# Layer 0 of a hybrid trunk: another split of the small inverses over the partitions, a written DMA order, and factors begun earlier

## The chip, the cores and the metric

The kernel runs on one core of one Trainium2 chip. The core has a matrix engine (TensorE, here PE), a vector engine (VectorE, DVE), a scalar engine (ScalarE, ACT), a slower general engine (GpSimd, POOL) and a queue that issues transfers (SyncE, SP). Each works off its own instructions in order, and they meet through semaphores. Transfers are done by 16 DMA engines. The metric is the device time of one execution in microseconds (us); lower is better.

## What is computed

Two layers run over 512 prompt tokens and 32 sample tokens (T = 544 columns). Layer 0 is an RWKV-7 mixer, layer 1 differential attention. Each layer also attends to a memory of 256 rows, gates its output and projects it back. Layer 0 is where the change lies. For each of 24 heads, reference and kernel follow the recurrence

```python
def step(S, inp):
    r_t, k_t, v_t, w_t, kk_t, a_t = inp
    sa = jnp.einsum('bhvk,bhk->bhv', S, -kk_t)
    S = (S * w_t[:, :, None, :] + sa[..., None] * (kk_t * a_t)[:, :, None, :]
         + v_t[..., None] * k_t[:, :, None, :])
    return S, jnp.einsum('bhvk,bhk->bhv', S, r_t)
```

with r, k, v, w, kk and a taken from the projection `h @ rw_in` (1024 rows) and its shift by one token. Afterwards come a group norm, the gate `silu`, and `x + out @ w_out`.

## The kernel before

**Tiling.** The 24 heads are handled as 12 pairs (128 partitions each). Tokens are cut into chunks of 64: eight for the prompt, a ninth for the sample. Inside a chunk the recurrence becomes matrix products, which need the inverse of a triangular 64x64 matrix per head and chunk. It is built from 32x32 blocks: 32 blocks per pair for the prompt and 2 for the sample, 34 in all (`NBLK`).

**Stages of a pair**, each a generator that is advanced one segment at a time by `go(kind, pr)`:

- `prep` (`rw_prep`): from the projections k, r, v it makes the decays, the factors `zr` and `bk`, the products `at` and `ats` (PE, tiles `ps_at`, `ps_ats`), and writes the blocks to be inverted to a scratch in device memory (`sc1`, L637 and L639). From there it loads them three times into `m3` (L641), once for each of three classes of rows.
- `inv` (`rw_invert`): POOL inverts all blocks together. `m3`, `u3` and `tm` are tiles of 3x34 = 102 partitions; 62 instructions (L689, L691) on tiles of falling size, after a copy of the unit matrix into `u3` (L683).
- `back` (`rw_back`): `u3` goes to a scratch `sc2` (L699, three transfers), and from there into `at` (L706) and `ats` (L708).
- `mrg` (`rw_merge`): DVE transposes blocks of `at` into `t1b`; PE makes `ps_w` from them (two rounds), which joins 32x32 inverses into 64x64 ones.
- `val`, `chain`, `smp`, `out`, `fin`: products with v, the eight chunks one after the other (three segments each, called hops below: PE, DVE, PE, ACT, PE, DVE, with psum tile `ps_c`), the sample's chunk, the outputs and the group norm.

**Dense work.** All projections (k, r, v, gates, queries, memory) run as blocks of 48 PE instructions on `ps_g` (24 for a memory block). A value is split into a high and a low half (`whi`, `wlo`), and three products are added up. `stream()` yields these blocks one instruction at a time. At the start of block i it issues the load of block i+2 (`raw`, L262) and puts the splitting of block i+1 on a list of put-off work, which `some()` takes from.

**Order.** While `self.ordered` is set, the instructions of PE, DVE and ACT are tied to program order (`Queue`, `tie`); transfers and POOL are not, and the framework's scheduler places them. Before the first chain there is a ramp: `FILL0` and `FILL1` say how many dense instructions follow each segment of `prep` of pairs 0 and 1 (384 in the whole ramp). Then for each pair there are 23 steps of one hop each, and `PLAN` says what else goes into the two halves of each step: (kind, which pair counted from this one, PE time, DVE time). The dense instructions left for the pair (192 in most, 144 in pair 0, 96 in pair 9, 240 in pairs 10 and 11) are spread evenly over planned PE time.

What matters below of the `PLAN` before, by step: `inv` of the next pair at step 1, `back` at step 13, `mrg` at 18, 19 and 21. `prep` of the pair after next begins at step 0, reaches `ats` at step 20, and its last four segments are taken in the next pair.

Of the kernel before, what the change touches and what calls it, by code (L numbers as in the profile page):

```python
# [33 lines left out]
RKV = 5  # L34
# [11 lines left out]
    [[("val", 0, 1.1, 0)], [("prep", 2, 0, 0), ("fin", -1, 0, 1.0)]],  # L46
    [[("prep", 1, 0.25, 0)], [("inv", 1, 0, 0), ("fin", -1, 0, 0.84)]],
    [[("prep", 1, 0.4, 0), ("fin", -1, 0, 0)], [("prep", 2, 0, 0.6)]],
    [[("val", 0, 0.8, 0)], [("fin", -1, 0, 0.98)]],
    [[("prep", 2, 1.04, 0.17), ("out", -1, 0.11, 0)], [("prep", 1, 0.53, 0)]],  # L50
    [[("prep", 2, 0.33, 0)], [("rsq", 0, 0, 1.5)]],
    [[("prep", 2, 0.33, 0), ("prep", 1, 0.4, 0)], [("prep", 2, 0, 0.1), ("fin", -1, 0, 0.88)]],
    [[("prep", 2, 0, 1.45)], [("prep", 2, 0.33, 0)]],
    [[("prep", 2, 0.33, 0), ("fin", -1, 0.6, 1.0)], [("prep", 2, 0, 0.5)]],
    [[("prep", 2, 0.1, 0), ("prep", 2, 0, 0)], []],
    [[("prep", 2, 0, 0.42)], [("prep", 2, 0, 1.04)]],
    [[("prep", 2, 0.56, 1.0), ("smp", 0, 0.11, 0.28)], []],
    [[("prep", 2, 0, 1.0), ("smp", 0, 0.21, 0.29)], [("prep", 2, 0, 0.86)]],
    [[("prep", 2, 0, 0.84)], [("back", 1, 0, 0)]],
    [[("prep", 2, 0, 1.1), ("smp", 0, 0.21, 0)], [("fin", -1, 0, 0.73)]],  # L60
    [[("prep", 2, 0, 0.86)], []],
    [[("prep", 2, 1.1, 1.37)], []],
    [[("prep", 2, 0, 0.9)], []],
# [4 lines left out]
    [[("out", 0, 1.6, 0.7)], [("prep", 2, 0.36, 0.43)]]]  # L68
# [5 lines left out]
             + [(10.5 + k, 4) for k in range(10)]}  # L74

FILL0 = [8, 4, 10, 0, 4, 4, 10, 2, 2, 2, 2, 8, 4, 8, 8, 8, 6, 6, 8, 8, 10, 6, 10, 6, 4, 4, 4, 4, 4, 4]
FILL1 = 6
FILLE = [20, 8, 8, 8, 10, 12, 10, 8]
# [19 lines left out]
class Trunk:  # L98
# [82 lines left out]
    def consts_rwkv(self, c):  # L181
# [44 lines left out]
        self.ve.tensor_scalar(cls[:], cl[:], float(NBLK), None, ALU.is_ge)  # L226
        for k in range(2, NCL):
            cl2 = c.tile([NCL * NBLK, 1], F32, name=f"cl2{k}")
            self.ve.tensor_scalar(cl2[:], cl[:], float(k * NBLK), None, ALU.is_ge)
            self.ve.tensor_tensor(cls[:], cls[:], cl2[:], ALU.add)  # L230
# [25 lines left out]
    def load(self, src, c0):  # L256

        h = KT // 2
        raws = []
        for q in range(2):  # L260
            raw = self.wp.tile([P, h, P], F32, tag="raw", name="raw", bufs=RAWS)
            self.nc.sync.dma_start(raw[:], src[q * h * P : (q + 1) * h * P, c0 : c0 + P].rearrange("(k p) c -> p k c", p=P))  # L262
            raws.append(raw)
        return raws
# [30 lines left out]
    def some(self, room):  # L295

        us = 0.0
        if self.later and 0 < self.later[0][1] <= room:
            fn, us = self.later.pop(0)
            fn()  # L300
        if self.later and self.later[0][1] == 0:
            self.later.pop(0)[0]()
        return us
# [39 lines left out]
    def inputs(self):  # L343

        nc, a = self.nc, self.a
        with ExitStack() as ctx:
# [3 lines left out]
            for i in range(2):  # L350
                nc.sync.dma_start(xt[5 + i][:], a["mem_prompt"][0, i * P : i * P + P, :])
            parB = self.params(p, "pB", [(a[n].rearrange("l (j p) -> (l j) p", p=P), 16) for n in ("norm_w", "mem_norm_w")])
            self.early = [self.load(a["w_mem_k"][0], h * P) for h in range(NEARLY)]
            for i in range(4):
                nc.sync.dma_start(xt[i][:], a["x_prompt"][0, i * P : i * P + P, :])
            nc.sync.dma_start(xt[4][:TS, :], a["x_sample"][0])
# [39 lines left out]
            for k in range(0, KT, 2):  # L396
# [8 lines left out]
                nc.sync.dma_start(self.mscr[k // 2], mo[:])  # L405
# [74 lines left out]
    def load_up(self, pr):  # L480

        self.up = up = self.rp.tile([P, 2, P], F32, tag="r4", name="up", bufs=1)
        for q, n in enumerate(("rw_w_up", "rw_a_up")):
            for rows in (slice(0, 64), slice(64, P)):
                self.nc.sync.dma_start(up[rows, q, :], self.a[n][0, :, pr * P : pr * P + P])

    def rw_prep(self, st, rkv):
# [46 lines left out]
        self.ve.tensor_tensor_scan(cum[:, :CU], self.smask[:, :CU], cum[:, :CU], 0.0, ALU.mult, ALU.add)  # L534
        yield
# [3 lines left out]
        yield  # L539
        rr = self.rr  # L540
        self.ve.tensor_copy(rr[:, :10], self.r20[:, :10])
        self.ve.tensor_tensor(rr[:, 10:20], self.r20[:, :10], rr[:, :10].bitcast(F32), ALU.subtract)
        yield
# [5 lines left out]
        de = p.tile([P, CW], F32, tag="de", name="de", bufs=1)  # L549
        di = cum  # L550
        self.ae.activation(de[:, :CU], cum[:, :CU], AF.Exp, scale=-KAPPA)
        self.ae.activation(di[:, :CU], cum[:, :CU], AF.Exp, scale=KAPPA)
        yield
# [3 lines left out]

        kf = p.tile([P, T], F32, tag="tmp", name="kf", bufs=2)
        self.ae.activation(kf[:], ta[:], AF.Identity, bias=col(self.omka), scale=col(self.ka2))
        na = p.tile([P, T], F32, tag="tmp", name="na", bufs=2)  # L560
        self.ae.activation(na[:], ta[:], AF.Copy, bias=-0.5, scale=-0.5)
# [19 lines left out]
        for q, c0, n in ((0, 0, TP), (1, TP, TS)):  # L581
            psb = self.psm.tile([P, 512], F32, tag="m", name="ps_b")
            for i in range(4) if q == 0 else (4,):
# [3 lines left out]
                                         ALU.mult, ALU.mult)  # L587
        yield
        decayed(zr, 1, nk, de, 0)
# [12 lines left out]
        st["ats"] = ats = self.rb.tile([P, 2, 2, 64], F32, tag="ats", name="ats", bufs=2)  # L602
# [20 lines left out]
        yield  # L623
        ps = [self.psm.tile([P, 512], F32, tag="m", name="ps_ats") for _ in range(2)]
# [6 lines left out]
        st["m3"] = m3 = self.rb.tile([NCL * NBLK, 32, 32], F32, tag="m3", name="m3", bufs=1)  # L631
        sc1 = self.dp.tile([NBLK, 32, 32], F32, tag="sc1", name="sc1", bufs=2)
        for e in range(2):
            for b in range(2):
                o = (64 if e == 0 else 0) + 32 * b
                n = (e * 2 + b) * 8
                nc.sync.dma_start(sc1[n : n + 8].rearrange("b s t -> s b t"),  # L637
                                  at[o : o + 32, e, 1 - e].rearrange("p i h t -> p (i h) t")[:, :, 32 * b : 32 * b + 32])
        nc.sync.dma_start(sc1[32:34].rearrange("h s t -> s h t"), ats[64:96, 1, :, :32])  # L639
        for q in range(NCL):  # L640
            nc.sync.dma_start(m3[q * NBLK : (q + 1) * NBLK], sc1[:])  # L641
# [18 lines left out]
        for q in range(2):  # L660
            yield
            if q:
# [4 lines left out]
                for u in range(2):  # L667
                    sv[u] = self.rb.tile([P, 4, P], F32, tag="sv", name="sv", bufs=4)
# [10 lines left out]
    def rw_invert(self, st):  # L679

        nc, p, m3 = self.nc, self.rb, st["m3"]
# [11 lines left out]
    def rw_back(self, st):  # L693

        nc, u3, at, ats = self.nc, st["u3"], st["at"], st["ats"]
        sc2 = self.dp.tile([NBLK, 32, 32], F32, tag="sc2", name="sc2", bufs=2)
        for q in range(NCL):
            n = len(range(q, 32, NCL))
            d = nc.sync.dma_start(sc2[:, q : 32 : NCL, :], u3[q * NBLK : (q + 1) * NBLK, :n, :])  # L699
            self.order(d, self.te.last)  # L700
        for e in range(2):
            o = 64 if e == 0 else 0
            for b in range(2):
                n = (e * 2 + b) * 8
                u = slice(o + 32 * b, o + 32 * b + 32)
                nc.sync.dma_start(at[u, e, 1 - e].rearrange("p i h t -> p (i h) t")[:, :, 32 * b : 32 * b + 32],  # L706
                                  sc2[n : n + 8].rearrange("b s t -> s b t"))
        nc.sync.dma_start(ats[64:96, 1, :, :32], sc2[32:34].rearrange("h s t -> s h t"))  # L708
# [56 lines left out]
    def chunk(self, st, c, S, Snew):  # L765
# [17 lines left out]
        for h in range(2):  # L783
            self.ae.copy(cv[zs, H[h]], ps[H[h], 1, H[h]])
        yield
# [22 lines left out]
    def rw_sample(self, st):  # L808
# [3 lines left out]
        for h in range(2):  # L812
            nc.sync.dma_start(sl[64 * h : 64 * h + 64, 64 * h : 64 * h + 64], self.a["state_rwkv"][0, 0, 2 * pr + h])
# [20 lines left out]
    def state_out(self, S, dst):  # L834
# [7 lines left out]
        nc.sync.dma_start(dst.rearrange("h v k -> (h v) k"), so[:])  # L842
# [31 lines left out]
    def put(self, g, t):  # L874
        if not self.o1:
            self.nc.sync.dma_start(self.oscr[g // 8][:, g % 8, :], t[:])
# [47 lines left out]
    def mem_again(self, mh, ml):  # L924
# [3 lines left out]
        for k in range(KT + 2):  # L928
            if k < KT:
                mo[k] = p.tile([P, NMEM], F32, tag="memo", name="mo", bufs=2)  # L930
                self.nc.sync.dma_start(mo[k][:], self.mscr[k // 2][:, k % 2, :])
# [14 lines left out]
    def mem_out(self, i, kind, h, t, out, ps_pool, ps_tag):  # L946

        nc, p, scr = self.nc, self.mp, self.mem[i, kind][h]
        if kind == 0:
            nc.sync.dma_start(scr[:], t[:])  # L950
# [5 lines left out]
        nc.sync.dma_start(out[:, h, :].rearrange("(j p) d -> p j d", p=P), tok[:])  # L956
        if kind == 1:
            nc.sync.dma_start(scr[:].rearrange("p (j c) -> p j c", j=2), tok[:])
# [9 lines left out]
    def mem_block(self, i, kind, h, mh, ml, w, out, ps_pool, ps_tag):  # L968
# [5 lines left out]
        for k in range(KT):  # L974
            for u, x in ((0, mh), (0, ml), (1, mh)):
                end = k == KT - 1 and u == 1
                self.te.matmul(ps[:, :NMEM], w[u][:, k, :], x[:, k, :], start=k == 0 and x is mh and u == 0, stop=end)
                if end:
                    self.ae.copy(t[:], ps[:, :NMEM])
                    self.open.append(None)  # L980
                    self.put_off(lambda: self.mem_out(i, kind, h, t, out, ps_pool, ps_tag))
# [35 lines left out]
    def mem_steps(self, st, i, h, p):  # L1017
# [7 lines left out]
        nc.sync.dma_start(ct[:], a["cache_mem_k"][i, 0, :, h, :].rearrange("(j p) d -> p j d", p=P))  # L1025
        nc.sync.dma_start(mk[:], self.mem[i, 0][h][:])
        nc.sync.dma_start(mv[:], self.mem[i, 1][h][:].rearrange("p (j c) -> p j c", j=2))
        nc.sync.dma_start(cv[:], a["cache_mem_v"][i, 0, :, h, :].rearrange("(j p) d -> p j d", p=P))
# [68 lines left out]
    def w_out(self, i, p, order, consume, extra=None):  # L1097
# [3 lines left out]
        for g in order:  # L1101
            if self.o1:
                t = self.o1[g]
            else:
                t = p.tile([P, T], F32, tag="os", name="os", bufs=OSB)
                nc.sync.dma_start(t[:], self.oscr[g // 8][:, g % 8, :])
# [48 lines left out]
    def layer0(self, mem):  # L1155
# [6 lines left out]
        with ExitStack() as ctx:  # L1162
# [22 lines left out]
            def go(kind, pr):  # L1185
# [3 lines left out]
                elif 0 <= pr < NPAIR:  # L1189
                    if kind in ("inv", "back"):  # L1190
# [510 lines left out]
```

## Time and profile before

| | |
|---|---|
| median of 3 timed runs | 1698.08 us (1694.68 to 1702.46) |
| profiled execution: its own time | 1687.72 us |
| its span, first to last instruction | 1685.9 us |
| PE busy | 1495.1 us (89%) |
| DVE, ACT, POOL busy | 900.8, 820.2, 376.4 us |
| mean granted PE clock | 0.93 |

The profile is of one execution. A row of the "windows" view gives, for a stretch of time, each engine's busy us with its number of instructions, the clock granted to PE (1.00 is full), the share of the 16 DMA engines that was busy, and GB/s. A row of the "waits" view reads: engine and tile that waited, what ended the wait, us in total, number of times, longest. The chain of waits follows the work back from the end, each piece with its start and length. The columns of the SP rows are start, length, queue, line, transfer and count. Marks of the first `yt` copy on ACT date the start of each pair's chain: 161.5, 213.7, 280.7, 346.4, 412.0, ..., 671.8, 735.9, 804.6, 860.8 us for pairs 0 to 11.

### The profile page before, as it was taken

How to read it: one execution, taken by the hardware profiler on the slowest of the kernel's cores; microseconds unless marked ns; L12 is line 12 of the kernel's file. 1: busy time of each engine (PE TensorE's matmuls, PEld its weight loads, DVE VectorE, ACT ScalarE, POOL GpSimd, SP SyncE). 2: the span in 40 equal slices, each digit the busy share in tenths (PEclk: the TensorE clock that was granted, in tenths of full speed). 3: DMA queues.
4: the chain of work that ended last, by engine and by line, in shares of the span. 5: the costliest groups of instructions: out<-in, count | busy, mean ns of one | idle time of the engine just before them, and what ended most of it. 6: DMA issues, size and time to landing. Idle time of an engine off the chain costs nothing.

```text
span 1685.9 us, 32077 instructions
## 1 busy us (share of the span) xinstructions
PE 1495.1 (89%) x12112; PEld 1393.5 (83%) x12112; DVE 900.8 (53%) x2209; ACT 820.2 (49%) x2257; POOL 376.4 (22%) x843
## 2 busy tenths in 40 slices
PE   6986897797787877976998899899999999999997
PEld 6885786787777777865897899899998999989997
DVE  7562564664655655744566422654645564456533
ACT  6553563463563553642555422565446644565422
POOL 2033451642633623623500000310000100100000
PEclk9997897887987987977999999999999999999999
DMA  6422112112122121121323733523233222322321
GB/s 210 130 85 52 45 48 63 43 55 54 47 66 49 44 74 45 46 61 33 99 86 111 228 106 98 161 82 91 73 96 93 77 86 76 89 82 73 90 86 72
DMA packets 265381, 139.20 MB, mean 83 GB/s; under 512 B 56506, under 2 KB 255427, under 8 KB 265227
## 3 DMA queue, kind: packets, MB, share of 16 engines
q1 hardware_dynamic: 265226, 137.15, 28.8%
q8 instruction: 96, 1.57, 0.4%
q14 instruction: 59, 0.48, 0.1%
HBM read 110.98 MB, written 22.78 MB: 79 GB/s over the span
## 4 chain that ended last, share of the span: by engine, by line
PE 57%; POOL 18%; DMA 12%; issue 4%; DVE 3%; ACT 3%; SPq 3%; DVEq 0%; POOLq 0%; ACTq 0%
PE ps_g L95 38%; POOL u L691 9%; POOL tm L689 8%; DMA m<-sc 5%; DMA sc<-u 4%; PE ps_c L95 2%; PE ps_w L95 2%; PE ps_o L95 2%; PE ps_s L95 2%; DMA at<-sc 1%; PE ps_mm L95 1%; SPq L699 1%; PE ps_mo L95 1%; PE ps_v L95 1%; DVE wlo L95 1%
## 5 line engine op out<-in xcount | busy, mean ns | idle before, releaser
L95 PE MATMUL ps_g<-hh,whi 128*128 128x272 f32 x1808 | 550.9, 305 | 0.1
L95 PE MATMUL ps_g<-hh,wlo 128*128 128x272 f32 x1808 | 539.1, 298 | 0.2 <-DVE wlo L95 0.2
L95 PE MATMUL ps_g<-hl,whi 128*128 128x272 f32 x1808 | 538.1, 298 | 0.0
L95 DVE TENSOR_TENSOR wlo<-raw,whi 128x512 fp32r<-128x512 f32 x322 | 224.2, 707 | 259.7 <-ACT whi L95 256.2
L95 PEld LDWEIGHTS ps_g<-hh,whi 128*128 128x128 f32 x1808 | 348.2, 193 | 6.5 <-issue 0.6
L95 PEld LDWEIGHTS ps_g<-hl,whi 128*128 128x128 f32 x1808 | 347.6, 192 | 1.9
L95 PEld LDWEIGHTS ps_g<-hh,wlo 128*128 128x128 f32 x1808 | 347.2, 192 | 1.5 <-issue 0.6
L95 ACT CAST whi<-raw 128x512 fp32r<-128x512 f32 x322 | 193.5, 617 | 218.8 <-PE ps_g L95 164.1
L689 POOL TENSOR_TENSOR tm<-u,m 102x84 f32<-102x84 f32 (+23 forms) x372 | 151.5, 407 | 318.9 <-DMA m<-sc 215.5
L691 POOL TENSOR_TENSOR u<-u,tm 102x84 f32<-102x84 f32 (+23 forms) x372 | 162.3, 436 | 29.1
L95 PE MATMUL ps_g<-hi,whi 128*128 128x272 f32 x512 | 149.7, 295 | 5.3 <-ACT hi L95 5.3
L95 PE MATMUL ps_g<-lo,whi 128*128 128x272 f32 x512 | 149.7, 294 | 1.7 <-DVE lo L95 1.7
L95 PE MATMUL ps_g<-hi,wlo 128*128 128x272 f32 x512 | 149.8, 293 | 0.0
L1536 POOL TENSOR_TENSOR kz<-k,kh 64x544 fp32r<-64x544 f32 x24 | 32.6, 1357 | 415.8 <-ACT kh L95 414.8
L95 PE MATMUL ps_w<-t1b,at 32*32 32x32 f32 x384 | 22.6, 230 | 101.4 <-DVE t1b L95 101.3
L95 PEld LDWEIGHTS ps_w<-t1b,at 32*32 32x32 f32 x384 | 20.6, 143 | 104.1 <-DVE t1b L95 103.8
L95 PEld LDWEIGHTS ps_g<-hi,whi 128*128 128x128 f32 x512 | 98.2, 193 | 6.4 <-ACT hi L95 6.2
L95 PEld LDWEIGHTS ps_g<-lo,whi 128*128 128x128 f32 x512 | 98.8, 193 | 2.6 <-DVE lo L95 2.6
L95 PEld LDWEIGHTS ps_g<-hi,wlo 128*128 128x128 f32 x512 | 99.0, 193 | 0.0
L95 ACT COPY wm<-ps_w 32x256 f32<-32x256 f32 x24 | 8.7, 363 | 138.2 <-PE ps_w L95 138.0
L95 ACT COPY yt<-ps_c 64x128 f32<-64x128 f32 x96 | 24.9, 259 | 102.9 <-DVE avz L95 101.2
L95 DVE SCALAR_TENSOR_TENSOR SB<-ps_c,dl,sd 64x64 f32<-64x64 f32 x168 | 47.0, 280 | 46.0 <-PE ps_c L95 44.3
(362 smaller groups left out, 2763.9 us busy)
## 6 DMA issues: line engine op xcount, KB each, us to landing
raw<-in_rw_in_dram SPq DMA_DIRECT2D x114, 256.0 KB
raw<-in_df_in_dram SPq DMA_DIRECT2D x112, 256.0 KB
raw<-in_w_out_dram SPq DMA_DIRECT2D x64, 256.0 KB
m<-sc SPq DMA_DIRECT2D x36, 136.0 KB
oscr<-sg SPq DMA_DIRECT2D x16, 272.0 KB
os<-oscr SPq DMA_DIRECT2D x16, 272.0 KB
raw<-in_w_mem_k_dram SPq DMA_DIRECT2D x16, 256.0 KB
raw<-in_w_mem_v_dram SPq DMA_DIRECT2D x16, 256.0 KB
```

The costliest lines, as they stand in the source:

```text
L95: return lambda *a, **k: self.trunk.tie(self, issue(*a, **k))
L689: nc.gpsimd.tensor_tensor(tm[:, :n, :wd], u3[:, :n, kx : kx + 1].to_broadcast(sh), m3[:, kx : kx + 1, kx + 1 :].to_broadcast(sh), ALU.mult)
L691: nc.gpsimd.tensor_tensor(u3[:, :n, kx + 1 :], u3[:, :n, kx + 1 :], tm[:, :n, :wd], ALU.add)
L699: d = nc.sync.dma_start(sc2[:, q : 32 : NCL, :], u3[q * NBLK : (q + 1) * NBLK, :n, :])
L1536: nc.gpsimd.tensor_tensor(kz[rows[m], m, :], k[rows[m], :], hi.bitcast(F32), ALU.subtract)
```

## The change

- **Blocks.** The classes lie on partitions as 3x32 prompt blocks (0 to 95) and 3x2 sample blocks (96 to 101) where they were 3x34. `m3` is loaded by six transfers (three of 32 partitions, three of 2), and `sc2` written by six. The load of `m3` moves from the end of `prep` into `rw_invert`. `cls`, the class of each partition, takes a few more tiny DVE instructions once.
- **DMA queue.** All transfers go through a fourth `Queue`, `self.se`, so that in the ordered part SP works in program order too. `rw_back` is cut in two: `back` (u3 to sc2) and `at` (sc2 to at and ats).
- **Plan.** `inv` of the pair after next at step 12, `back` of the next pair at step 9, `at` at 11, `mrg` at 16, 17 and 20. `prep` begins at step 13 three pairs ahead (11 segments), continues as `prep` two ahead (18 segments, `ats` at step 11, first half) and ends as one ahead (3). `rw_prep` has 32 segments where it had 30, and some of its parts change places.
- **Ramp.** Four fill lists over `prep` of pair 0 (32 segments), of pair 1 (29), of pair 2 (11), and the merge; again 384 dense instructions. Blocks are reordered so that k and r of pair 1 come before two of the memory blocks; k of pair p+3 comes before the gate of pair p-1.
- **Smaller.** `RKV` 5 to 4 (buffers of k, r, v); in a hop the copies to `yt` and `sd` come after the copies to `cv`; the second `ps_b` uses another psum pool; `some()` keeps put-off work apart.

```diff
-RKV = 5
+RKV = 4
...
-    [[("prep", 1, 0.25, 0)], [("inv", 1, 0, 0), ("fin", -1, 0, 0.84)]],
...
-    [[("prep", 2, 0, 0.84)], [("back", 1, 0, 0)]],
...
-    [[("prep", 2, 1.1, 1.37)], [("mrg", 1, 0, 0.86)]],
-    [[("mrg", 1, 0.9, 0)], []],
-    [[("prep", 2, 0.5, 0.58), ("smp", 0, 0.6, 0.85)], []],
-    [[("mrg", 1, 0.9, 0), ("val", 1, 0.45, 0)], [("prep", 2, 0.36, 0.43), ("smp", 0, 0.11, 0)]],
...
+    [[("prep", 2, 1.1, 1.37)], [("back", 1, 0, 0)]],
+    [[("smp", 0, 0.6, 0.85)], []],
+    [[("prep", 2, 0.5, 0.58)], [("at", 1, 0, 0), ("fin", -1, 0, 1.0)]],
+    [[("prep", 2, 0.36, 0.43)], [("inv", 2, 0, 0), ("fin", -1, 0, 0.84)]],
+    [[("prep", 2, 0.36, 0.43)], [("fin", -1, 0, 0), ("prep", 3, 0, 0)]],
...
+    [[("prep", 3, 1.04, 0.17)], [("mrg", 1, 0, 0.86)]],
+    [[("mrg", 1, 0.9, 0)], [("rsq", 0, 0, 1.5)]],
...
+    [[("prep", 3, 0.33, 0), ("mrg", 1, 0.9, 0)], [("prep", 3, 0.33, 0), ("fin", -1, 0, 0.73)]],
...
-            self.nc.sync.dma_start(t[r0 : r0 + n, :], src)
+            self.se.dma_start(t[r0 : r0 + n, :], src)
...
-        us = 0.0
-        if self.later and 0 < self.later[0][1] <= room:
+        us, self.place_no = 0.0, self.place_no + 1
+        if len(self.later) > 4:
+            room = LATER
+        if self.later and 0 < self.later[0][1] <= room and self.place_no > self.acted + 1:
...
-        for q in range(NCL):
-            nc.sync.dma_start(m3[q * NBLK : (q + 1) * NBLK], sc1[:])
...
+        m3 = p.tile([NCL * NBLK, 32, 32], F32, tag="m3", name="m3", bufs=1)
+        for q in range(NCL):
+            self.se.dma_start(m3[q * 32 : q * 32 + 32], sc1[:32])
+            self.se.dma_start(m3[96 + 2 * q : 98 + 2 * q], sc1[32:])
...
-            d = nc.sync.dma_start(sc2[:, q : 32 : NCL, :], u3[q * NBLK : (q + 1) * NBLK, :n, :])
-            self.order(d, self.te.last)
+            for b, o, m in ((0, q * 32, 32), (32, 96 + 2 * q, 2)):
+                self.se.dma_start(sc2[b : b + m, q : 32 : NCL, :], u3[o : o + m, :n, :])
+
+    def rw_at(self, st):
...
-            self.ae.copy(yt[ro, i, :], ps[ro, 0, :])
-            sd = self.rb.tile([P, P], F32, tag="sd", name="sd", bufs=RB)
-            self.ae.activation(sd[:], S[:], AF.Copy, scale=st["dl"][:, c : c + 1])
             yield
...
         for h in range(2):
             self.ae.copy(cv[zs, H[h]], ps[H[h], 1, H[h]])
+        if c:
             self.ae.copy(yt[ro, i, :], ps[ro, 0, :])
+            sd = self.rb.tile([P, P], F32, tag="sd", name="sd", bufs=RB)
+            self.ae.activation(sd[:], S[:], AF.Copy, scale=st["dl"][:, c : c + 1])
...
+            blocks[2:6] = blocks[4:6] + blocks[2:4]
             for pr in range(10):
+                if pr + 3 < NPAIR:
+                    add_shift(pr, pr + 3, 1)
                 if pr:
                     rw_gate(pr, pr - 1)
...
+            go("back", 0)
+            for k, n in enumerate(FILL2):
+                go("prep", 2)
+                if k == 2:
+                    go("rsq", 2)
+                if k == 3:
+                    go("at", 0)
+                    go("inv", 1)
+                fill(n)
```

More of the change, by code (lines that the diff above doesn't have):

```diff
@@ L69 @@
+    [[("prep", 3, 0.33, 0)], [("prep", 3, 0, 0.1), ("fin", -1, 0.6, 1.0)]],
+    [[("prep", 3, 0.33, 0), ("mrg", 1, 0.9, 0)], [("prep", 3, 0.33, 0), ("fin", -1, 0, 0.73)]],
+    [[("prep", 3, 0, 1.45), ("val", 1, 0.45, 0)], [("prep", 3, 0, 0.5)]],
+    [[("out", 0, 1.6, 0.7)], [("prep", 3, 0, 0)]]]
 MEMPE = 4.8
@@ L1287, in layer0 @@
                     go("rsq", 0)
-                if k == 23:
+                if k == 25:
                     go("inv", 0)
+                fill(n)
+            for k, n in enumerate(FILL1):
+                go("prep", 1)
+                if k == 2:
+                    go("rsq", 1)
                 fill(n)
@@ L1298, in layer0 @@
             self.at.append(self.rb2.tile([P, 2, 2, 4, 2, 64], F32, name="at2"))
[L1299 to L1300 removed]
+            go("back", 0)
+            for k, n in enumerate(FILL2):
+                go("prep", 2)
                 if k == 2:
[L1302 to L1307 removed]
+                    go("rsq", 2)
+                if k == 3:
+                    go("at", 0)
+                    go("inv", 1)
+                fill(n)
+            for kind, n in zip(("mrg", "mrg", "val", "mrg"), FILL3):
                 go(kind, 0)
[L1309 to L1310 removed]
+                fill(n)
             for pr in range(NPAIR):
@@ L1344, in layer0 @@
                 if pr + 3 == NPAIR:
-                    for _ in range(4):
+                    for _ in range(3):
                         go("prep", pr + 2)
```

177 lines of the change are left out of this document (86 added, 91 removed), and 2 rows, old and new, of the table MPLAN.

## The prediction

> **What bounds the kernel now.** I read the page first, for the share of PE and its clock over time.
>
> ```profile
> span 1685.9 us, 32077 instructions
> ...
> PE   6986897797787877976998899899999999999997
> ...
> PEclk9997897887987987977999999999999999999999
> ```
>
> A slice is 42 us. From the 23rd slice on (about 930 us, the end of layer 0's ordered part) PE is full and its clock stays up. Before it, both dip about every 65 us. What the change moves lies there, so I asked for the waits of PE, and for windows cut at the marks of the pairs.
>
> ```profile
> PE ps_w L95 <- DVE t1b L95: 101.3, 12, 14.2
> PE ps_rt L95 <- DVE rr L95: 8.4, 8, 1.2
> PE ps_si L95 <- DVE nk L95: 8.3, 10, 1.2
> PE ps_v L95 <- ACT so L95: 6.7, 9, 1.6
> ```
>
> ```profile
> 100.50:134.40 33.90, 29.98 (x229) 28.10 (x227) 20.97 (x47) 14.76 (x36) 20.63 (x49) 0.95 0.17 51
> 134.40:161.50 27.10, 12.91 (x137) 12.09 (x137) 2.83 (x5) 5.76 (x16) 3.84 (x14) 0.69 0.28 68
> 161.50:213.70 52.20, 44.97 (x362) 40.62 (x364) 28.55 (x75) 30.24 (x89) 24.53 (x63) 0.86 0.18 44
> ...
> 213.70:735.90 522.20, 426.61 (x3760) 393.83 (x3760) 298.30 (x729) 258.76 (x752) 221.48 (x504) 0.86 0.21 54
> ...
> 804.60:860.80 56.20, 55.95 (x497) 51.74 (x498) 33.24 (x83) 29.94 (x96) 23.09 (x62) 1.00 0.36 101
> ```
>
> One wait towers over all others: 12 times, once per pair, PE stands in the merge for the transposed blocks, 101.3 us in all. Pairs 1 to 8 take 522.2 / 8 = 65.3 us each. Pair 10, which waits for nothing, does 497 PE instructions in 56.2 us at clock 1.00; the eight pairs average 470 and take 9 us longer. The chain of waits shows what t1b waits for:
>
> ```profile
> 272.57 0.73 PE ps_ats L95 x4
> ...
> 280.71 0.59 SPq L813
> ...
> 282.15 9.67 DMA m<-sc
> 291.98 0.25 POOL tm L689
> ...
> 323.41 0.25 POOL u L691
> 324.28 0.27 SPq L699
> ...
> 325.99 5.90 DMA sc<-u
> 332.03 1.61 DMA at<-sc
> 333.67 0.45 DVE t1b L95
> ...
> 338.27 0.73 PE ps_ats L95 x4
> ```
>
> This is a closed loop. From `ats` of one pair to its `t1b` 333.7 - 272.6 = 61.1 us pass: 9.6 until the last load of m is issued (SP stands at L813 for a piece of it), 9.8 for the load, 31.7 on POOL, 10.0 through two transfers. PE then merges, and the next pair's `ats` comes 4.6 us later. 61.1 + 4.6 = 65.7 us, which is the period. In the plan `ats` stands at step 20 and the merge at step 18 of the next pair, 21 steps on; they can't be shorter than the loop. So a latency through SP, DMA and POOL sets the pace, and PE pays for it twice:
>
> ```profile
> 346.40:349.00 2.60, 2.60 (x34) 2.37 (x35) 1.59 (x4) 0.30 (x1) 0.00 (x0) 0.54 0.11 30
> 349.00:391.00 42.00, 39.54 (x333) 37.22 (x331) 30.42 (x74) 26.74 (x77) 27.37 (x62) 1.00 0.16 47
> 391.00:399.90 8.90, 0.09 (x2) 0.04 (x2) 0.76 (x2) 0.00 (x0) 0.48 (x1) 0.62 0.40 87
> 399.90:412.00 12.10, 12.10 (x102) 10.28 (x104) 4.39 (x13) 5.32 (x16) 0.00 (x0) 0.50 0.25 60
> ...
> 412.00:415.00 3.00, 3.00 (x42) 2.73 (x43) 2.06 (x6) 0.56 (x4) 0.00 (x0) 0.72 0.08 16
> 415.00:456.60 41.60, 38.76 (x328) 36.64 (x326) 30.17 (x73) 26.51 (x76) 26.92 (x62) 1.00 0.16 47
> 456.60:466.00 9.40, 0.03 (x1) 0.03 (x2) 0.69 (x2) 0.00 (x0) 0.48 (x1) 0.76 0.38 82
> 466.00:476.60 10.60, 10.60 (x132) 8.99 (x132) 4.63 (x13) 5.28 (x17) 0.00 (x0) 0.73 0.30 69
> ```
>
> These are the pairs of marks 346.4 and 412.0, whole. In each, some 9 us are empty, and the work after the gap runs at a clock of 0.50 to 0.73.
>
> **The change, part by part.**
>
> *The loop is opened.* In the new plan `ats` stands at step 11 and the merge's transposes at step 16 of the next pair, second half: 23 + 5 = 28 steps and more. Its length, worked out: `ats` to sc1 landed, about 2 us, and SP's five `at` transfers queued between; then six loads of m; POOL; six transfers to sc2; five to `at`. What SP needs to issue them:
>
> ```profile
> 281.47 0.97 SPq L641 DMA_DIRECT2D m<-sc  x3
> ...
> 324.28 3.76 SPq L699 DMA_DIRECT2D sc<-u  x3
> ...
> 332.03 1.80 SPq L706 DMA_DIRECT2D at<-sc  x4
> ...
> 334.37 1.91 SPq L637 DMA_DIRECT2D sc<-at  x4
> ```
>
> With 0.3 us per issue of m, six take 1.9; four and one `at` take 2.3, the same again for sc1. The time of the six loads isn't in the trace. Below it is bounded by the 1.61 us of at<-sc (32 partitions as well), above by today's 9.67 plus 0.97 for three more issues, 10.6. For sc<-u the bounds are 1.6 and 5.9 + 3.8. I take 4 and 5, nearer to at<-sc, since the big piece now covers 32 partitions as there. Sum: 2 + 2.3 + 2.3 + 4 + 31.7 + 5 + 2.3 + 1.6 + 0.4 = 52 us; with both upper bounds 63.
>
> 28 steps at s us each must hold this. If PE alone sets the pace (51 us a pair, below), s = 51 / 23 = 2.2 and the 28 steps last 62 us. So the loop has 10 us to spare; with both upper bounds it lacks 1, and the period becomes 63 x 23 / 28 = 52. That is robust: to bring back 65.3 us the loop would have to last 79.5.
>
> POOL by itself: 31.7 + 4 + 5, since m3 and u3 have one buffer each, is 41 us per pair, under 51. DVE has 298.30 / 8 = 37.3 us per pair, ACT 32.3; both fit.
>
> *What a pair then takes.* In the pair of 346.4 the 42.0 us at full clock stay; 8.9 go; 12.1 at 0.50 become 6.1, and 2.6 at 0.54 become 1.4: 49.5. In the pair of 412.0: 41.6 + 3.0 x 0.72 + 10.6 x 0.73 = 51.5. The long stretches hold small waits (2.5 us of the 42). The hops of a chain at full clock say the same:
>
> ```profile
> 283.54 0.59 PE L95 MATMUL ps_c<-avz,at 128*128 128x128 f32 x2
> ...
> 317.00 0.45 PE L95 MATMUL ps_c<-avz,at 128*128 128x128 f32 x2
> ```
>
> Between these lie 15 hops in 33.5 us, 2.23 each; times 23 is 51.3. I take 51. The upper bound from pair 10, 56, counts more dense work; the lower, 49.5, is the pair above.
>
> *The sum*, against the profiled execution (span 1685.9, own time 1687.7):
>
> - Pairs 1 to 8: 522.2 to 8 x 51 = 408, less 114.
> - Pair 9 has half the dense work and the longest wait:
>
> ```profile
> 735.90:774.60 38.70, 32.54 (x254) 29.38 (x250) 27.66 (x72) 22.59 (x67) 23.25 (x55) 0.91 0.12 35
> 774.60:786.80 12.20, 0.07 (x2) 0.08 (x3) 1.31 (x3) 0.00 (x0) 2.18 (x9) 0.68 0.21 42
> 786.80:804.60 17.80, 15.83 (x145) 12.54 (x146) 6.76 (x19) 7.39 (x22) 0.00 (x0) 0.65 0.20 51
> ```
>
>   38.7 x 0.91 + 17.8 x 0.65 = 46.8, and 5 segments of `prep` fall into earlier pairs: 45. Of 68.7, less 24.
> - Pair 0: 52.2 x 0.86 = 45, plus 1 for 35 segments of `prep` where 30 were: less 6.
> - Ramp: from 134.4 to 161.5, the wait of 14.2 goes, the other 12.9 at 0.69 become 9: less 18. It gains 11 segments of pair 2 and 3 of pair 1. The 33.9 us row has 26 segments, 1.3 us each, of which six dense instructions take 0.75 and are only moved:
>
> ```profile
> 1136.08 10.43 PE ps_g L95 x83
> ```
>
>   10.43 / 83 is 0.126 each. 14 x 0.55 to 14 x 1.3 is 8 to 18, and I take 10, since dense work fills some of it. Less 8.
> - Pairs 10 and 11, the output projection and layer 1: no wait of theirs is touched. Zero.
>
> Together less 152: 1536 us for the profiled execution. That execution was 10.4 us under the median of the runs, so against 1698 I say **1546 us**.
>
> *Costed at nothing:* the reordered copies in a hop, the split `prep` and the second `ps_b` pool. They aim at the waits for rr, nk and so above, 23 us in all, from zero to 23 less; I take none of it, because denser DVE work may bring as many. RKV 4 makes r of pair p+3 reuse k of pair p+2, last read at step 8 while r is written after step 11; with less cover ACT's copy would wait a step, 2 us a pair.
>
> *DMA order.* Behind a waiting `back` on SP stand the loads of weights, and behind those PE's dense work. POOL ends about step 12.5 + (2.3 + 4 + 31.7) / 2.2 = 30, so step 7 of the next pair; `back` stands at 9.5. It waits for nothing, with 5 us of room; even 10 us would be covered by the block already in SBUF (48 x 0.126, and with the hops between some 12 us).
>
> **Rivals.**
>
> *The half clock stays, for want of dense work.* Only 102 instructions fill those 12.1 us, 8 per us, most of them merges and chains; pair 0 runs at 0.86 without a long wait. If the clock follows density and not the gap, the pairs keep their slow stretch: 51 + 6 = 57 for pairs 1 to 8, 5 each for pairs 0 and 9: 58 more, 1604. Against it: the new plan moves the end of `prep` to the middle of the pair and leaves dense work round the merges. [...] No row here separates the two.
>
> *SP's written order starves PE: slower.* Place: the load L262 behind `back` L699. If POOL ends over 17 us later than counted, one block is used up and PE waits in the dense work, once per pair. Price as for pair 9: 12.2 us empty and about 7 of lost clock, 51 + 19 = 70 a pair, 4.7 over now, and nothing won elsewhere: 1698 + 38 = 1736. Against it speaks that POOL's 31.7 us were taken beside a dense stretch already.
>
> *POOL and DVE exclude each other.* 37.3 + 27.7 us (221.48 / 8) are 65 a pair, as now, and the other terms go the same way: about 1695. In the 42.0 us row they were busy 30.42 + 27.37 us together, so at least 16 us overlapped. [...]
>
> *The transfers don't get shorter.* Then the loop is 63 us, 52 a pair: 1546 + 8 = 1554.
>
> **Chances.** Forecast 0.66 (own range 1523, if the small waits go, to 1570); half clock 0.20; transfers 0.06; exclusion 0.03; starving 0.05. Under 0.5% (8.5 us) this measurement can't be told from no change. Faster 0.92, same 0.03, slower 0.05. The range 1518 to 1625 holds the first three.
>
> **What would show it.** Right: `ps_w` no longer waits for `t1b`; the marks of pairs lie 49 to 53 us apart; clock near 1.00 from 160 us on; POOL ends before SP reaches L699. Wrong in steps: m loads of 8 us or more; slow clock around merges with no gap (second case); long waits of `ps_g` for `wlo` with SP held at the u transfers (third); POOL's inversion over 40 us (fourth). If the marks stay 65 us apart, my loop isn't what sets the pace.

## The result, and the profile after

The changed kernel takes 1506.86 us (median of 4 runs, 1505.41 to 1511.37) against 1697.65 us: a ratio of 0.8878, 95% interval 0.8850 to 0.8907. That is 191 us less. The prediction was faster, 1546 us, with a range of 1518 to 1625. It had the direction right, and a loop of transfers and POOL as what set the pace. Its gain of 152 us is a fifth too small, and the measured time lies 11 us below the range. The profiled execution took 1505.4 us.

The page of the changed kernel, the same lines as shown of before:

```profile
span 1503.7 us, 32159 instructions
...
PE   5999999999999998999899989999999999999997
...
PEclk9999999999999999999999989999999999999999
```

Only the first slice still starves. The waits of PE over the whole run:

```profile
PE ps_par L96 <- DMA pB<-in_mem_norm_w_dram: 6.3, 1, 6.3
...
PE ps_rt L96 <- DVE rr L96: 1.2, 1, 1.2
...
PE ps_w L96 <- DVE t1b L96: 0.6, 2, 0.4
```

The wait for t1b fell from 101.3 us to 0.6, and the small waits (rr, nk, so: 23 us before) went with it. The windows of the changed kernel, cut at its own marks: ramp, pair 0, pairs 1 to 8, one of these by itself, pair 9.

```profile
64.00:143.20 79.20, 73.98 (x645) 68.40 (x644) 50.51 (x119) 46.77 (x114) 30.03 (x78) 1.00 0.39 106
143.20:190.80 47.60, 44.40 (x414) 41.12 (x414) 31.10 (x79) 30.24 (x89) 30.12 (x75) 0.93 0.21 51
190.80:578.00 387.20, 382.44 (x3714) 359.81 (x3713) 293.58 (x726) 261.58 (x750) 225.46 (x513) 0.99 0.28 72
335.90:383.70 47.80, 47.32 (x468) 44.53 (x468) 36.62 (x92) 32.76 (x95) 26.78 (x62) 1.00 0.28 74
578.00:618.80 40.80, 35.54 (x363) 31.54 (x363) 31.12 (x81) 25.09 (x77) 23.01 (x58) 1.00 0.18 43
```

Pairs 1 to 8 take 387.2 / 8 = 48.4 us each, and PE is busy for 47.3 of the 47.8 in the pair shown alone. PE is the bound now. The ramp of the kernel before, for comparison:

```profile
64.00:161.50 97.50, 74.79 (x623) 69.67 (x622) 46.17 (x104) 41.29 (x100) 24.94 (x67) 0.89 0.30 82
```

By the terms of the sum, in us:

| term | before | after | measured | predicted |
|---|---|---|---|---|
| ramp, to the mark of pair 0 | 161.5 | 143.2 | -18.3 | -8 |
| pair 0 | 52.2 | 47.6 | -4.6 | -6 |
| pairs 1 to 8 | 522.2 | 387.2 | -135.0 | -114 |
| pair 9 | 68.7 | 40.8 | -27.9 | -24 |
| from the mark of pair 10 to the end | 881.3 | 884.9 | +3.6 | 0 |
| sum | 1685.9 | 1503.7 | -182.2 | -152 |

The medians differ by 191 and not by 182 since the profiled execution of before was 10 us under its median and that of the changed kernel 1.5.

### The profile page after: what moved, and what is told of

Its sections match the earlier page's. It is cut to its first block, busy times and chain, and to the rows that moved or that the text cites. A ratio compares the mean times of both kernels' runs of the same rounds, so it can differ in the third digit from the quotient of the medians.

```text
span 1503.7 us, 32159 instructions
## 1 busy us (share of the span) xinstructions
PE 1437.1 (96%) x12112; PEld 1347.2 (90%) x12112; DVE 897.8 (60%) x2223; ACT 824.4 (55%) x2257; POOL 379.5 (25%) x843
## 4 chain that ended last, share of the span: by engine, by line
PE 78%; DVE 6%; ACT 5%; DMA 4%; POOL 4%; issue 2%; SPq 2%; DVEq 0%; ACTq 0%; POOLq 0%
PE ps_g L96 54%; PE ps_c L96 4%; PE ps_s L96 2%; PE ps_o L96 2%; PE ps_v L96 2%; POOL u L700 2%; SPq L96 2%; POOL tm L698 2%; PE ps_at L96 1%; PE ps_w L96 1%; PE ps_mm L96 1%; PE ps_mo L96 1%; DVE wlo L96 1%; ACT whi L96 1%; PE ps_aT L96 1%
## 5 line engine op out<-in xcount | busy, mean ns | idle before, releaser
L96 PE MATMUL ps_g<-hh,whi 128*128 128x272 f32 x1808 | 544.9, 301 | 0.1
L698 POOL TENSOR_TENSOR tm<-u,m 102x84 f32<-102x84 f32 (+23 forms) x372 | 161.3, 434 | 204.3 <-DMA m<-sc 176.2
L700 POOL TENSOR_TENSOR u<-u,tm 102x84 f32<-102x84 f32 (+23 forms) x372 | 152.7, 411 | 29.1
L1442 POOL TENSOR_TENSOR hl<-hn,hh 128x544 fp32r<-128x544 f32 x8 | 11.9, 1523 | 237.7 <-ACT hh L96 237.7
L96 ACT ACTIVATE pt<-ps_s,snm 128x128 f32<-128x128 f32 (+3 forms) x96 | 50.7, 530 | 22.3 <-DVE snm L96 21.9
L96 ACT COPY raw<-ps_g 128x272 f32<-128x272 f32 x74 | 28.6, 387 | 56.7 <-PE ps_g L96 56.3
L96 DVE TENSOR_REDUCE snm<-ps_s 128x1 f32<-128x128 f32 (+3 forms) x96 | 46.1, 488 | 19.9 <-PE ps_s L96 17.8
```

Source lines behind the costliest of these rows:

```text
L96: return lambda *a, **k: self.trunk.tie(self, issue(*a, **k))
L698: nc.gpsimd.tensor_tensor(tm[:, :n, :wd], u3[:, :n, kx : kx + 1].to_broadcast(sh), m3[:, kx : kx + 1, kx + 1 :].to_broadcast(sh), ALU.mult)
L700: nc.gpsimd.tensor_tensor(u3[:, :n, kx + 1 :], u3[:, :n, kx + 1 :], tm[:, :n, :wd], ALU.add)
L1442: nc.gpsimd.tensor_tensor(self.hl[:, k, :], h[:], self.hh[:, k, :].bitcast(F32), ALU.subtract)
```

## Experiments

The loop of the prediction (ats, load of m, POOL, transfers, merge) had three parts of the change working on it at once. Experiments 1 to 4 take these apart, 6 and 7 measure the room that is left, 5 and 8 to 12 ask where the small waits went. All changes of a time are against the median of the kernel before on the same chip, or against 1506.9 us for variants of the changed kernel.

### 1. The kernel before, blocks as 32 and 2

```diff
-            nc.sync.dma_start(m3[q * NBLK : (q + 1) * NBLK], sc1[:])
+            nc.sync.dma_start(m3[q * 32 : q * 32 + 32], sc1[:32])
+            nc.sync.dma_start(m3[96 + 2 * q : 98 + 2 * q], sc1[32:])
...
-            d = nc.sync.dma_start(sc2[:, q : 32 : NCL, :], u3[q * NBLK : (q + 1) * NBLK, :n, :])
-            self.order(d, self.te.last)
+            for b, o, m in ((0, q * 32, 32), (32, 96 + 2 * q, 2)):
+                d = nc.sync.dma_start(sc2[b : b + m, q : 32 : NCL, :], u3[o : o + m, :n, :])
+                self.order(d, self.te.last)
```

> The kernel before with one part of the change: the blocks lie as 32 and 2 per class, so m is loaded and sc2 written by six transfers. Plan and DMA order stay. Loop theory (a pair lasts as long as the closed loop ats, load of m, POOL, two transfers, merge): in the kernel before the load takes 10.5 us from its first issue to POOL and the way from POOL's last instruction to the end of sc<-u 8.4; in the changed kernel they take 4.6 (363.1 to 367.7) and about 4.3. So the loop loses 5.9 + 4.1 = 10 of 65.7 us, a pair takes 56, and with ramp and pair 9 the time falls by about 10 x 10 = 100 us, to some 1600 us. Rival (what counts is how dense work lies around the merges, not the loop): plan unchanged, so under 20 us of gain, about 1685 us.

Measured: 1562.5 us (ratio 0.919, 0.916 to 0.922), 135.6 less. Both theories missed: the loop theory was right in direction and too timid. Two pairs of this run, the second and the seventh:

```profile
203.90:259.90 56.00, 52.93 (x470) 48.59 (x472) 37.20 (x92) 32.41 (x95) 28.19 (x63) 0.90 0.27 70
...
470.80:522.00 51.20, 48.02 (x471) 44.48 (x466) 37.52 (x92) 32.25 (x94) 28.38 (x63) 1.00 0.27 68
```

Pairs 1 and 2 take the 56 us that were expected, pair 3 takes 52.4, and from pair 4 on pairs settle at 51.2 with full clock. That the first two agree with the expectation is luck: PE is busy for 52.9 of the 56 us, its longest wait for t1b is 0.8 us, and what fills the pair is a stretch at a lower clock around the merge, here that of pair 1:

```profile
249.00:262.00 13.00, 12.53 (x133) 10.72 (x134) 5.99 (x17) 5.64 (x17) 0.44 (x2) 0.61 0.40 102
```

One reason why the settled pairs gain more than the 10 us lies in the loop itself, which runs through PE for a stretch. The chain of waits from the merge to the instruction that the next state load waits for, before and then in this run:

```profile
334.16 2.03 PE ps_w L95 x32
...
341.75 1.66 PE ps_w L95 x32
...
345.87 0.44 PE ps_c L95 x2
```

```profile
462.67 1.15 PE ps_w L95 x31
...
467.01 1.02 PE ps_w L95 x32
...
469.58 0.22 PE ps_c L95 x2
```

The same work takes 12.1 us before (334.2 to 346.3), at a clock of 0.50 behind a gap, and 7.1 here (462.7 to 469.8), at 1.00 and with no gap. So the half clock lengthened the loop too: it slowed the very instructions that start the next load. In the settled pairs both are gone. That the gap alone brings the half clock isn't shown, since in the row of 249.00 the clock falls behind a wait of no more than 0.8 us. With an unchanged plan, this part alone brings 136 of the 191 us.

### 2. The same, and SP in program order

Every transfer of the kernel of experiment 1 goes through a fourth queue, `self.se`, tied as the others are.

> As the run before it, and also SP in program order; the plan stays, so factors are not begun earlier. Loop theory: in the kernel before, m waits 5 us in SP's queue behind the state load (276 to 281.5); in program order it comes right behind sc1. The loop falls to about 51 us, near the 48 that PE needs, so pairs take 51 to 52 and the time is about 1560 us: the earlier start of the factors would then be worth only the last 50 us. Rival (SP's written order starves PE): back stands at step 13 while POOL ends at about step 18, the loads of weights wait behind it for 10 us a pair, and the time is no better than with blocks alone, 1600 us or more.

Measured: 1554.6 us (0.916, 0.913 to 0.919). A pair in the settled part:

```profile
463.80:515.00 51.20, 48.15 (x473) 44.61 (x469) 37.07 (x92) 32.38 (x96) 25.60 (x63) 1.00 0.27 69
```

The loop theory said 51 to 52 us a pair and 1560 us in all; pairs settle at 51.2 from pair 4 on, the first three take 53.4 to 54.8, and the time is 1555. But experiment 1 settles at 51.2 without the written order, and the intervals of the two ratios overlap, so these runs don't show that the order shortened the loop. `back` at step 13 didn't starve PE of weights; the rival of the prediction in which SP's order does so is out for this plan too.

### 3. The changed kernel, blocks back at 34

The reverse of the first edit, three loads of m and three writes of sc2, in the changed kernel.

> The changed kernel with the blocks back at 34 per class: three loads of m, three writes of sc2. The theory of the prediction (28 steps must hold the loop, 63 us with slow transfers): 52 us a pair, 4 over the 48.4 measured, 9 pairs, about 1543 us. Second theory, from the changed kernel's SP rows (POOL and SP form a cycle of their own, since with one m3 and a written order the next load of m stands behind sc<-u and at<-sc): 31.4 on POOL + 9.0 to sc2 landed + 2.4 for at + 10.5 for m = 53.3 a pair, about 1551 us. Third (the transfers had room, PE sets the pace): 1507 us. The SP rows decide between the first two: in the second, POOL waits for nothing but m, and at<-sc is issued the moment sc2 has landed.

Measured: 1574.8 us (0.927, 0.925 to 0.929), 68 more than with 32 and 2. The waits of PE, the windows of pairs 1 to 8, and then POOL's and SP's rows between two inversions:

```profile
PE ps_w L96 <- DVE t1b L96: 40.9, 11, 6.0
```

```profile
210.60:635.70 425.10, 395.09 (x3715) 372.74 (x3714) 293.87 (x726) 262.01 (x751) 206.56 (x506) 0.95 0.26 66
```

```profile
501.73 0.23 POOL L699 TENSOR_TENSOR u<-u,tm 102x11 f32<-102x11 f32 x1
...
509.84 0.48 POOL L691 CAST u<-ui 102x352 f32<-102x352 bf16 x1 [7.88 <-DMA sc<-u]
...
525.64 0.24 POOL L697 TENSOR_TENSOR tm<-u,m 102x31 f32<-102x31 f32 x1 [15.32 <-DMA raw<-in_rw_in_dram]
...
501.98 3.75 SPq L96 DMA_DIRECT2D sc<-u  x3
...
510.76 2.94 SPq L96 DMA_DIRECT2D at<-sc  x4
...
514.25 0.92 SPq L96 DMA_DIRECT2D m<-sc  x3
```

A pair takes 425.1 / 8 = 53.1 us; the second theory said 53.3, that of the prediction 52. The rows bear out the second: SP goes straight from one transfer to the next, and from 501.96 to 525.64, 23.7 us, POOL does nothing but one copy of 0.48 us. (The releaser named is a load of weights that landed last; the load of m was issued 11.4 us before.) So even with factors begun a third of a pair earlier, slow transfers set the pace. The total rose by more than the 44 us expected; with 143.2 to 154.9 for the ramp and 47.6 to 55.7 for pair 0, these held another 20. Read against the kernel before, this run has everything of the change but the blocks and is 123 us faster. The blocks alone bring 136 (experiment 1), both together 191: each of the two opens much of the loop, so their gains don't add up.

### 4. The changed kernel, SP's order free

`self.se` is SyncE itself, with no tie.

> The changed kernel with SP no longer tied to program order; blocks and plan as changed. Theory (the plan leaves room in the loop, the order only spares a few us): the scheduler may put m behind a state load or a store for some 5 us a pair, which the cycle of 43.7 us against 48.4 just about holds: 1507 to 1530 us. Rival (the written order is what makes the plan work, because otherwise sc<-u or m wait behind loads of weights whose buffers are not free, up to 15 us in the kernel before): the merge waits again, 8 us or more a pair, 1580 us and up.

Measured: 1512.6 us (0.891, 0.889 to 0.893), 5.8 more. Ramp and pairs 1 to 8:

```profile
64.00:149.20 85.20, 77.20 (x642) 71.37 (x642) 51.08 (x119) 47.54 (x115) 30.30 (x80) 0.95 0.35 95
196.60:585.40 388.80, 383.87 (x3714) 361.20 (x3713) 294.01 (x726) 261.27 (x750) 220.79 (x522) 0.98 0.28 72
```

48.6 us a pair against 48.4. The written order is worth some 6 us, if that: the interval of the ratio overlaps with that of the changed kernel (0.8850 to 0.8907). In the two profiled executions the difference stands in the ramp (85.2 against 79.2); the pairs don't need the order. The rival falls.

### 5. The changed kernel, four small edits undone

The copies to `yt` and `sd` first in a hop, one psum pool for both `ps_b`, put-off work by the old rule, and in `prep` scan before the second tanh and the transposed `r` before the exponentials.

> The changed kernel with four small edits undone together: the copies to yt and sd come before those to cv again, both ps_b in one psum pool, put-off work taken as before, and in prep the order of scan, second tanh, transposed r and exponentials as before. The prediction took 51 us a pair, of which 2.5 to 3 were small waits of PE carried over from the kernel before; measured were 48.4 with 0.5 us idle. If these edits removed the waits, they come back: 2 to 2.5 us a pair, about 1525 to 1530 us, with ps_rt on rr (8.4 before) and ps_c on yt (6.2 before) among the waits. If the new plan removed them, by what stands between producer and consumer: under 5 us, 1507 to 1512 us.

Measured: 1544.9 us (0.912, 0.910 to 0.914), 38 more. Pairs 1 to 8, and their waits of PE:

```profile
199.20:611.10 411.90, 384.67 (x3732) 358.62 (x3732) 293.33 (x729) 264.75 (x750) 212.75 (x507) 1.00 0.26 68
```

```profile
PE ps_c L96 <- DVE SB L96: 11.0, 14, 1.4
PE ps_so L96 <- ACT svs L96: 5.5, 8, 0.7
PE ps_w L96 <- DVE bv L96: 5.0, 7, 0.7
PE ps_b L96 <- ACT sv L96: 4.3, 7, 1.0
```

411.9 / 8 = 51.5 us: 3.1 more per pair, 25 us over eight; pair 9 and the ramp hold most of the rest. The first theory's sign is right, but not its size (18 to 23 us) and not its waits. Those on rr stayed away in these pairs, and others came in their place.

### 6 and 7. POOL made longer by 5 and by 11 us

```diff
             wd = 31 - kx
+            for _ in range(9 if kx == 30 else 0):   # 20 in the second
+                nc.gpsimd.tensor_copy(tm[:], self.ui[:])
```

> The changed kernel with 9 more POOL copies of about 0.48 us (0.55 with the gap) before the last step of each inversion, into a tile that is overwritten right after: 5 us longer on POOL, the result is the same. Theory of the prediction (10 us to spare in 28 steps): no change, 1507 us. Second theory (cycle of POOL and SP, 43.7 us, of 47.8): 48.7 a pair, 1 us over, about 1515 us.

> The same with 20 copies, 11 us longer on POOL. Theory of the prediction: 62 us of steps against a loop of 63, at most 1 us a pair, 1507 to 1516 us. Second theory: 54.7 us a pair, 6.5 to 7 over, 9 to 10 pairs, about 1568 us, and POOL idle only for SP and DMA, some 12 us between two inversions. Rival of the prediction (SP held at sc<-u starves PE of weights): waits of ps_g for wlo appear in the middle of blocks.

Measured: 1540.1 us (0.909, 0.906 to 0.912) and 1621.5 us (0.956, 0.954 to 0.959). Windows of pairs 1 to 8 of the first, of the second, and rows of POOL and SP between two inversions in the second, then the same place in the changed kernel:

```profile
200.10:606.40 406.30, 390.52 (x3715) 368.21 (x3714) 296.70 (x727) 262.13 (x751) 263.59 (x580) 0.96 0.27 69
```

```profile
215.30:680.20 464.90, 399.66 (x3715) 377.23 (x3715) 300.64 (x728) 262.56 (x751) 318.03 (x666) 0.91 0.23 60
```

```profile
584.19 12.35 POOL L698 CAST tm<-ui 102x352 f32<-102x352 bf16 x20
...
596.91 0.23 POOL L702 TENSOR_TENSOR u<-u,tm 102x11 f32<-102x11 f32 x1
...
609.49 0.24 POOL L700 TENSOR_TENSOR tm<-u,m 102x31 f32<-102x31 f32 x1 [8.54 <-DMA m<-sc]
...
605.28 2.09 SPq L96 DMA_DIRECT2D m<-sc  x6
```

```profile
350.40 0.23 POOL L700 TENSOR_TENSOR u<-u,tm 102x11 f32<-102x11 f32 x1
...
354.07 0.70 POOL L692 CAST u<-ui 102x352 f32<-102x352 bf16 x1 [3.43 <-DMA sc<-u]
...
367.73 0.24 POOL L698 TENSOR_TENSOR tm<-u,m 102x31 f32<-102x31 f32 x1 [12.96 <-DMA m<-sc]
...
350.66 2.17 SPq L96 DMA_DIRECT2D sc<-u  x6
...
360.66 1.93 SPq L96 DMA_DIRECT2D at<-sc  x4
...
363.13 2.08 SPq L96 DMA_DIRECT2D m<-sc  x6
```

The prediction's room of 10 us is refuted: 5 more cost 33 us, and pairs go to 50.8 and 58.1 us. When POOL is late, 12.35 us lie between two inversions (597.14 to 609.49); in the changed kernel 17.1 (350.63 to 367.73). By these rows the room is 17.1 - 12.35 = 4.7 us, close to the second theory's 48 - 43.7. The periods say less: the copies took some 5.3 and 12.6 us a pair, and 50.8 - 5.3 and 58.1 - 12.6 both leave 45.5 for the cycle itself, so of the 48.4 about 3 us are room. The second theory has the mechanism, but its 1515 and 1568 us are 25 and 53 too low. The total rises by more than eight pairs' worth (8 x 2.4 = 19 and 8 x 9.7 = 78), since ramp, pair 0 and pair 9 lose too; the clock over pairs 1 to 8 falls to 0.96 and 0.91. Weights didn't starve: no wait of ps_g for wlo was longer than 1.9 us.

### 8. Everything but the new plan

The kernel of experiment 2 with the four small edits put in.

> The kernel before with blocks of 32 and 2, SP in program order, and the small edits (order of the copies in a hop, of scan, tanh, transposed r and exponentials in prep, second psum pool for ps_b, put-off work), but with its own plan, ramp, RKV and order of blocks: factors are not begun earlier. Blocks and SP order alone gave 1554.6 us, and its undisturbed pairs took 51.2 us with 3.1 idle. Theory A (the loop is open already, and the small edits bring the same 38 us here that they cost when undone in the changed kernel): about 1517 us, pairs of 48 to 49 us. Theory B (the small edits only work with the steps of the new plan, since a wait vanishes by what stands between): 1545 to 1555 us, pairs of 51. Between them, the new plan is worth what is left to 1507.

Measured: 1555.4 us (1544.6 to 1558.6; 0.915, 0.910 to 0.919): no gain over experiment 2 that the runs can tell. Theory B holds. The two leading waits of PE in pairs 1 to 8, and the windows of these pairs and of pair 9:

```profile
PE ps_rt L95 <- DVE rr L95: 15.9, 8, 2.0
PE ps_w L95 <- DVE t1b L95: 6.7, 9, 0.8
```

```profile
193.40:606.50 413.10, 388.79 (x3760) 365.70 (x3760) 297.37 (x730) 259.81 (x753) 215.07 (x504) 0.97 0.27 68
606.49:661.26 54.77, 44.83 (x396) 38.61 (x393) 35.98 (x91) 30.27 (x87) 32.24 (x82) 0.91 0.18 43
```

With the old plan the edits trade waits: those on nk go, the one on rr grows to 2.0 us in every pair. Given the small edits, the new plan, with its ramp, `RKV` and order of blocks, is worth 1555.4 - 1506.9 = 48 us. In the two profiled executions it is 39 (this one lies 11 us under its median): 26 in pairs 1 to 8 (413.1 against 387.2), where PE's idle time falls from 24.3 to 4.8 us and only 6.7 of it were for t1b, and 14 in pair 9 (54.8 against 40.8).

Experiments 2, 5 and 8 and the changed kernel form a square. With neither the new plan nor the small edits the time is 1554.6 us, with the plan alone 1544.9, with the edits alone 1555.4, with both 1506.9. Alone the plan brings 10 us, with intervals that overlap, and the edits nothing that the runs can tell; together they bring 48.

### 9 to 12. The small edits undone one by one

In the order hop copies, order in `prep`, rule for put-off work, psum pool of `ps_b`.

> The changed kernel with one of the four small edits undone: in a hop the copies to yt and sd stand in the first segment again. Undoing all four cost 38 us, and the waits then were ps_c on SB (11.0 us in pairs 1 to 8), ps_so on svs (5.5), ps_w on bv (5.0), ps_b on sv (4.3). If the hop is the cause of the waits on SB, because ACT is late with what SB needs: 10 to 25 us of the 38, 1517 to 1532 us. If not, 1507.

> The changed kernel with only the order inside prep undone (scan before the second tanh, transposed r before the exponentials). If the order in prep is the cause, since the plan's weights are made for it and the exponentials come right before the copy that waits for them: 10 to 25 us of the 38, 1517 to 1532 us; ps_rt on rr should then be among the waits. If not, 1507.

> The changed kernel with only the rule for put-off work undone. If two put-off pieces in neighbouring places hold up ACT or DVE in a hop: 5 to 20 us of the 38, 1512 to 1527 us. If not, 1507. The three runs and the second ps_b pool, which isn't run by itself, should add up to 38 if the edits don't act on the same waits.

> The changed kernel with the fourth small edit alone undone: both ps_b tiles lie in the psum pool of two buffers again. All four undone cost 38 us, the other three singly 5.7, 5.1 and 7.2, together 18. If the edits act on separate waits, this one costs the missing 20: about 1527 us, 2 us a pair, with PE waiting at ps_b or right after it. If the edits cover for each other (a wait shows only when two or more are undone): 1507 to 1512 us.

Measured: 1512.6, 1511.9, 1514.0 and 1509.2 us, so 5.7, 5.1, 7.2 and 2.3 more. Their ratios (0.892, 0.890, 0.891 and 0.887, intervals of about 0.003 to each side) overlap with that of the changed kernel, so no single step is shown to be clear of the measurement. Of the forecasts, 9 and 10 fell between their two branches (1507, and 1517 to 1532), 11 lies in its range, and 12 agrees with edits that cover for each other. Windows of pairs 1 to 8 of the first three, and for each of 9 and 12 the wait that came:

```profile
195.30:590.10 394.80, 384.72 (x3718) 360.63 (x3716) 293.84 (x729) 265.28 (x751) 214.71 (x506) 0.99 0.28 71
```

```profile
193.90:586.70 392.80, 385.37 (x3732) 360.90 (x3732) 294.95 (x729) 260.52 (x750) 218.28 (x510) 0.99 0.28 71
```

```profile
196.70:585.00 388.30, 382.16 (x3715) 358.30 (x3714) 292.46 (x727) 262.75 (x751) 226.89 (x505) 0.99 0.28 72
```

```profile
PE ps_so L96 <- ACT svs L96: 6.2, 9, 0.7
```

```profile
PE ps_b L96 <- ACT sv L96: 4.0, 8, 0.5
```

49.4, 49.1 and 48.5 us a pair, in executions that lie 4 to 9 us above their medians: none brings the waits on SB of experiment 5. Together the four give 20 us, undone at once 38. They cover for each other, and which of them together bring the wait on SB stays open.

## Where the prediction was right, and which steps failed

**The bound, right.** A closed loop per pair through transfers and POOL set the pace. Experiment 1 shows it by taking transfer time out of it. Experiments 3, 6 and 7 put time back, and show a shorter cycle of POOL, below.

**The half clock, right in outcome, its cause open.** It was forecast to go with the gaps, and in pairs 1 to 8 of the changed kernel both are gone (0.99); pair 0 still stands at 0.93. That the gaps alone caused it isn't shown: pair 1 of experiment 1 stands at 0.90, with no wait of PE over 1.2 us. The rival "half clock stays" is out as a forecast for the changed kernel, but its mechanism isn't: in the first pairs of experiment 1 the clock falls to 0.61 around the merge with no gap. What the clock follows is open.

**The loop opened by 28 steps: wrong in the room.** The step "the loop has 10 us to spare" counted SP's transfers once along one pair's loop. The tighter cycle is that of POOL: one m3, one u3, and the next load of m behind sc<-u and at<-sc on SP. The prediction put it at 41 us; measured are 43.7 by the rows and 45.5 by the periods, with a room of 3 to 4.7. It didn't decide, because PE needs 48.

**Loads of m and sc<-u: right.** Taken as 4 and 5 us, nearer to at<-sc. In the changed kernel the load of m takes 4.6 us from its first issue to POOL (363.1 to 367.7), where it was 10.5; sc<-u takes 3.4 us from POOL's end to the copy that waits for it (350.6 to 354.1), where the same wait was 7.8. The share of the DMA engines, the last figure but one, shows how differently the two loads ran. These are five microseconds of the load of m in the kernel before, and the whole load in the changed kernel:

```profile
350.00:355.00 5.00, 5.00 (x46) 4.88 (x44) 3.26 (x8) 3.89 (x9) 0.00 (x0) 1.00 0.13 49
```

```profile
363.20:367.70 4.50, 4.48 (x38) 4.24 (x37) 3.33 (x8) 4.36 (x12) 0.00 (x0) 1.00 0.40 106
```

With 34 partitions the share is 0.13, the busy time of 0.13 x 16 = 2 engines; with 32 and 2 it is 0.40, that of 0.40 x 16 = 6.4 on average over a row that holds the issues too. What in the split makes the difference isn't shown.

**51 us a pair: the step that failed.** Measured 48.4. The 51 is what the old plan costs once its loop is open: 51.2 in the settled pairs of experiments 1 and 2, close to what was read out of the trace of before. The step that failed is the one that costed the small edits "at nothing", with the small waits of 2.5 us per 42 carried over. The new plan and the small edits together took them away (0.5 us idle in the pair shown); by the square of experiment 8 neither does so alone. This is 21 of the 30 us by which the sum of 152 was short of 182. The prediction's own lower case, 1523 with the small waits gone, is still 16 us too high, and the next two terms fill that.

**The ramp: priced too dear.** 14 more segments of `prep` were put at 10 us. The ramp lasts 79.2 us where it lasted 97.5. PE's idle time in it fell from 22.7 to 5.2 us, so more than the wait of 14.2 went, and its busy time stayed (74.79 to 73.98). At the clocks of the prediction's two rows of the old ramp, 0.95 and 0.69, the old 74.79 would be some 69 at full clock, so the added segments cost PE about 5 us, an estimate. Off by 10.

**The step from profile to median.** The 10.4 us by which the profiled execution of before lies under its median were carried over to the changed kernel. It lies 1.5 under its own. That is another 9 us, and together with the other terms it put the time 11 us below the range.

**The rivals.** Starving by SP's order: none in any run; without the written order the time is some 6 us longer, with overlapping intervals. Exclusion of POOL and DVE, 65 us a pair: out, 48.4 are measured, and 293.58 + 225.46 us of busy time stand in 387.2 us. Transfers that don't get shorter: experiment 3 puts the old shapes back, which costs 68 us, not 8, by the cycle of POOL.

## What to carry to other kernels

When a wait on the matrix engine repeats with a period, walk the chain once round and ask which of its pieces run at a lower clock behind the wait: here a gap of 8.9 us (its row stands in the prediction) and the work behind it cost 14 us a pair, as this work took 12.1 us at a clock of 0.50 instead of 7.1 at 1.00. A transfer's partition count deserves a look before any plan is rewritten; the split into 32 and 2 alone gave 136 of 191 us, where all the rest without it gave 123. Small waits read out of the old order are a property of that order, so a new order can remove or add them, and the range should hold both. Parts of a change that look small alone can be worth their price only together: try them undone one by one and all at once.

## What was not expected

- The new start of the factors, the largest part of the edit, hardly acts through the loop once the blocks are 32 and 2: with them the old plan waits 6.7 us for t1b in eight pairs. Its gain stands in the other small waits, the clock of the pairs (0.99, where experiment 8 has 0.97) and pair 9, and nearly all of it needs the small edits.
- Pairs of one and the same program settle: in experiment 1, 56.0 us for pairs 1 and 2, 52.4 for pair 3, then 51.2, with the same waits listed. Why the first ones keep the lower clock is open.
